# Hybrid decoder layer on one core: the second tile's x and rows loaded one per step, the attention bias begun at another point

## The chip, the cores and the metric

The kernel runs on one core of a Trainium2 chip. The metric is the device time of one execution in microseconds (us). The core has five engines that run their own instruction streams: TensorE (PE, with weight loads listed apart as PEld), VectorE (DVE), ScalarE (ACT), GpSimd (POOL) and SyncE (SP), the last of which issues most of the DMA transfers here. Lines such as L127 are lines of the kernel's file before the change.

## The reference

One decoder layer on x of 2048 positions and 1024 channels, all float32:

```
hn   = rms_norm(x, mix_pre_g)
proj = hn @ w_in                       # 1024 -> 1792: q, k, v and u
attn = sliding_window_attention(q, k, v, attn_sinks, rel_bias)   # window 128, 8 heads of 64
conv = conformer_conv(u, ...)          # GLU, causal conv of 31 taps, layer norm, swish, pointwise
h    = x + rms_norm(concat(attn, conv) @ w_out, mix_post_g)
hf   = rms_norm(h, ffn_pre_g)
out  = h + rms_norm((silu(hf @ w_gate) * (hf @ w_up)) @ w_down, ffn_post_g)
```

The bias of attention is rel_bias (32 buckets by 8 heads) picked by the distance of query and key.

## The kernel before

**Precision.** Each float32 operand of a large product is split in a high half (an ACT copy to fp32r) and a low half (a subtraction on POOL or DVE), and each product is three products on PE: high by high, high by low, low by high (`three`, `split_w`).

**Tiles and stages.** The 2048 positions are four tiles of 512. Stage A (labels A0 to A3, `stage_a`) is the first projection of a tile: 14 units of 128 output columns, each of 8 blocks of 128 channels by three products, so 24 products of 128x512. Units 0 to 7 are the GLU pairs of the four convolution groups, 8 and 9 are k and v, 10 to 13 are q. Stage C (`stage_taps`) does the 31 convolution taps on DVE; stage B is attention; stages W, F, H and G are the output projection and the FFN. X (`stage_x`) makes the attention bias once; U (`stage_fold`) folds the pointwise weights into the output weights.

**How a unit's weights come.** `kweight` loads 512 KB of w_in into a tile of tag raw (two buffers), splits it in two halves (tag w, six buffers, so three units), and in the first tile stores the low halves to a scratch tensor lo_in (two stores of 256 KB), from which the later tiles read them. In the first tile units 0 to 5 are subtracted on POOL (`TAPS0 = 6`), the rest on DVE.

**How x comes.** The first tile's transposed x (label X0) is loaded at the very start. For the second tile, step 2 of A0 calls `h1`, which is `load_x`: four DMAs of 512 KB (tag x, four buffers, L262). Step 4 calls `h0`, which is `row_norms`: four DMAs of 512 KB of the rows of x (tag p, L276), a Square with a running sum on ACT for each (L277), and `rsqrt`, three small DVE instructions and twelve small ones on POOL (L153 to L156). Step 8 (`h2`) makes the diagonal matrix of the norms, step 10 (`h3`) transposes and copies it, steps 11 and 12 (`h4`, `h5`) scale and split the eight blocks of x for stage A1 (tags mid and chl).

**What sets the order.** The code below is emitted in program order with a priority; a planner then orders each engine's stream, SP's included, by that priority and a model of when the operands are ready. An instruction may thus stand in its stream far ahead of its place in the code when its buffers are free. A manual dependency marked NoSync orders two instructions in the plan and puts no semaphore between them; `tied` puts one on the last product so far. Side stages run in lanes: after every unit the main loop yields its cost (5.2) and `pump` gives each lane credit for it, at 0.8 for lane lb, with X first and B0 to B3 behind it. A lane's stage takes its next part when its credit is above zero, and its yields are taken off the credit. X starts when its condition holds, here that the second tile's x has been begun (`"x1" in started`).

Of the kernel before, what the change touches and what calls it, by code (L numbers as in the profile page):

```python
# [17 lines left out]
AF = mybir.ActivationFunctionType  # L18
# [5 lines left out]
D = 1024  # L24
DFF = 2816
P = 128
T = 512
# [10 lines left out]
def layer_kernel(ctx, tc, x, xT, cols, rows, sinks, relb, onehot, w_in, w_pw, w_out, w_gate, w_up, w_down, out):  # L38
    nc = tc.nc
# [7 lines left out]
    lab = ["X0"]  # L47

    def nm(s):
        uid[0] += 1  # L50
        return f"{s}@{lab[0]}_{uid[0]}"
# [3 lines left out]
    def t_(tag, shape, dt=F32):  # L55
        return sb.tile(list(shape), dt, tag=tag, name=nm(tag), bufs=BUFS[tag])

    def f4(tag, shape=(P, D)):
        return t_(tag, shape)

    def f2(tag, shape=(P, T)):
        return t_(tag, shape)
# [4 lines left out]
    def sm(n, dt=F32):  # L67
        kind = "A" if lab[0][0] == "G" else lab[0][0]
        return sb.tile([P, 8], dt, tag="sm" + kind, name=nm("sm"), bufs=16)[:, 0:n]
# [9 lines left out]
    act = nc.scalar.activation  # L79
# [4 lines left out]
    def mat(*args, **kw):  # L84
        r = nc.tensor.matmul(*args, **kw)  # L85
        if made["new"]:
            made.update(rows=[], at=0, new=False)
        made["rows"].append(r.ins)
        return r
# [54 lines left out]
    def rsqrt(ssq, n, mean_over, beside_taps=True):  # L144
        v = sm(n)
        y = sm(n)
        t = sm(n)
        vts(v, ssq, 1.0 / mean_over, EPS, ALU.mult, ALU.add)
        vts(y.bitcast(I32), v.bitcast(I32), 1, None, ALU.logical_shift_right)
        vts(y.bitcast(I32), y.bitcast(I32), -1, 0x5F3759DF, ALU.mult, ALU.add)  # L150
        for _ in range(3):
            if beside_taps:
                ptt(t, y, y, ALU.mult)  # L153
                ptt(t, t, v, ALU.mult)
                nc.gpsimd.tensor_scalar(t, t, -0.5, 1.5, ALU.mult, ALU.add)
                ptt(y, t, y, ALU.mult)  # L156
            else:
                vtt(t, y, y, ALU.mult)
                stt(t, v, -0.5, t, ALU.mult, ALU.mult)
                stt(y, t, 1.5, y, ALU.add, ALU.mult)  # L160
        return y
# [20 lines left out]
    def tied(r):  # L182
        tc.add_manual_dep(
            r.ins,
            made["rows"][-1].name,
            mybir.DependencyInfo(mybir.DependencyClass.NoSync, mybir.DependencyReason.DATA),
            reason="keeps pace with the products",
        )
        return r
# [56 lines left out]
    junk = cst.tile([P, D], BF16, name="junk")  # L246
# [8 lines left out]
    started = set()  # L255
# [9 lines left out]
        return [xs]  # L265

    rn = {}

    def row_norms(ts, tag):
        lab[0] = f"A{ts[0]}"  # L270
        n = 4 * len(ts)
        ssq = sm(n)
        for i in range(n):
            xt = f4(tag)
            r0 = ts[0] * T + i * P
            nc.sync.dma_start(xt, x[r0 : r0 + P])  # L276
            act(junk, xt, AF.Square, accum_out=ssq[:, i : i + 1])  # L277
        r = rsqrt(ssq, n, D)
        for j, t in enumerate(ts):
            rn[t] = r[:, 4 * j : 4 * j + 4]  # L280
# [13 lines left out]
    def norm_x(t, xs, acc):  # L294
        lab[0] = f"A{t}"
        bank_of = mm if t else ct
        if t:
            r = acc
        else:
            o = bank_of()  # L300
            for s in range(4):
                mat(o[:, s : s + 1], acc[:, s * P : (s + 1) * P], ones, start=True, stop=True)
            r = rsqrt(o[:, 0:4], 4, D, False)
        dg = f2("gb")
        for s in range(4):
            vts(dg[:, s * P : (s + 1) * P], ident, 0.0, r[:, s : s + 1], ALU.mult, ALU.add)
        yield
        lab[0] = f"A{t}"
        o = bank_of()
        for s in range(4):  # L310
            nc.tensor.transpose(o[:, s * P : (s + 1) * P], dg[:, s * P : (s + 1) * P], ident)
        rb = f2("gb")
        act(rb, o, AF.Copy)
        yield rb
# [336 lines left out]
    def stage_fold():  # L651
        lab[0] = "U0"

        def two(src):
            raw = f4("wx", (P, 2, T))
            nc.sync.dma_start(raw, src)
            return raw

        wp = []
        for i in range(2):  # L660
            lab[0] = "U0"
            raw = two(w_pw[2 * i : 2 * i + 2].rearrange("c p t -> p c t"))
            wp += [split_w(raw[:, j], "mid", on_pool=False) for j in range(2)]
            yield 2.76
        for n in range(2):
            wo = []
            for i in range(2):
                lab[0] = "U0"
                c = 4 + 2 * i
                raw = two(w_out[c : c + 2, :, n * T : (n + 1) * T].rearrange("c p t -> p c t"))  # L670
                wo += [split_w(raw[:, j], "chl", on_pool=False) for j in range(2)]
                yield 0.1 if n else 2.76
            for m in range(4):
                lab[0] = "U0"
                o = mm()
                ms = slice(m * P, (m + 1) * P)
                three(o, [((wp[j][:, 0, ms], wp[j][:, 1, ms]), (wo[j][:, 0], wo[j][:, 1])) for j in range(4)])
                f = hl("chl" if m % 2 else "mb")
                act(f[:, 0], o, AF.Copy)
                vtt(f[:, 1], o, f[:, 0].bitcast(F32), ALU.subtract)  # L680
                nc.sync.dma_start(fold[n, m], f.bitcast(F32))
                yield 2.76
# [3 lines left out]
    def stage_x():  # L686
        lab[0] = "X0"
        rel = cst.tile([32, 8], F32, name="rel")
        nc.sync.dma_start(rel, relb)
        oh = f2("fa", (P, 2 * P))  # L690
        nc.sync.dma_start(oh[0:32], onehot)
        pb = tr()
        mat(pb[0:8, 0 : 2 * P], rel, oh[0:32], start=True, stop=True)
        bs = f2("fa", (P, 2 * P))
        nc.vector.tensor_copy(bs[0:8], pb[0:8, 0 : 2 * P])
        b_scr = dr.tile([8, 2 * P], F32, name="b_scr")
        nc.sync.dma_start(b_scr, bs[0:8])
        yield 8
        lab[0] = "X0"
        flip = f2("fa", (P, P))  # L700
        nc.gpsimd.memset(flip, 0.0)
        nc.gpsimd.affine_select(
            out=flip, in_=flip, compare_op=ALU.not_equal, fill=1.0, base=1 - P, pattern=[[1, P]], channel_multiplier=1
        )
        up = t_("mb", (P, 8, P))
        nc.sync.dma_start(up, bass.AP(tensor=b_scr.tensor, offset=b_scr.offset, ap=[[1, P], [2 * P, 8], [1, P]]))
        yield 8
        lab[0] = "X0"
        t = t_("mb", (P, 8, P))
        for n in range(2):  # L710
            o = tr()
            mat(o, flip, up[:, 4 * n : 4 * n + 4].rearrange("p h k -> p (h k)"), start=True, stop=True)
            nc.vector.tensor_copy(t[:, 4 * n : 4 * n + 4].rearrange("p h k -> p (h k)"), o)
        bias.append(t)
        yield 0.1
# [673 lines left out]
    lb = Lane(RB, 0)  # L1389
# [19 lines left out]
    def mark(gen, name):  # L1409
        for c in gen:  # L1410
            yield c
            started.add(name)

    lb.add("X", stage_x(), lambda: "x1" in started)
    lu.add("U", stage_fold(), lambda: "A2" in started)
    lw.add("W0", stage_w(0, "x", ["hl"] * 4, ["wx"] * 4, mm), lambda: "A3" in started and "C0" in ld.done and "U" in lu.done)
    TGA = [["hl"] * 8, ["mid"] * 4 + ["chl"] * 4, ["hl"] * 8, ["mid"] * 4 + ["hl"] * 4]
    xa = {}
# [8 lines left out]
    for t in range(NT):  # L1427
        hooks = {}
        if t + 1 < NT:

            def h1(t=t + 1):
                xa[t] = load_x(t)

            def h3(t=t + 1):
                xa[t][2] = next(xa[t][2])

            def h4(t=t + 1):
                hn_a[t] = split_x(t, xa[t][0], xa[t][2], range(4))

            def h5(t=t + 1):  # L1440
                hn_a[t] += split_x(t, xa[t][0], xa[t][2], range(4, KC))

            def h0(t=t + 1):
                row_norms([t] if t == 1 else [2, 3], "p" if t == 1 else "hl")

            def h2(t=t + 1):
                xa[t] += [rn[t], norm_x(t, xa[t][0], rn[t])]
                next(xa[t][2])

            if t == 0:  # L1450
                hooks = {2: h1, 4: h0, 8: h2, 10: h3, 11: h4, 12: h5}
            elif t == 1:
                hooks = {0: h1, 2: h0, 7: h2, 9: h3, 10: h4, 11: h5}
            else:
                hooks = {H1: h1, H2: h2, H3: h3, H4: h4}
        run(mark(stage_a(t, hn_a[t], (lambda: lb.until(f"B{t-1}")) if t else (lambda: None), hooks,
                         None if t else norm_x(0, x0, sum_squares(0, x0))), f"A{t}"))
        lb.add(f"B{t}", stage_b(t))
        if t == 2:
            hn_a[t + 1] += split_x(t + 1, xa[t + 1][0], xa[t + 1][2], range(4, KC))  # L1460
# [97 lines left out]
```

## Time and profile before

| | us |
|---|---|
| median of 3 runs (1934.53 to 1942.58) | 1941.39 |
| the profiled execution | 1939.15 |
| its span in the profile | 1937.4 |
| PE busy in the span | 1897.0 |
| DVE busy in the span | 1475.7 |
| ACT busy in the span | 959.2 |
| POOL busy in the span | 310.2 |

The views of the profile are read like this. In a view of stretches each row is a stretch of the span with the busy time of each engine in it (and how many instructions), then the granted clock of TensorE as a share of full speed, the busy share of the DMA engines and the GB/s that they moved. In a view by time a row is the start, the duration, the engine, the line, the operation, the tile written and the tiles read, the shapes, the count, and in brackets how long the engine sat idle before it and what it waited for. In the view of waits a row is who waited for whom, with the total, the number of times and the longest. SPq marks what SP's queue issues. Between the label A0's first products and its last stand about 90 us of the span; the first large matrix product starts at 7.08 us.

### The profile page before, as it was taken

The page shows a single profiled execution, that of the slowest core. Times are in us where ns is not written, and L with a number is a line of the kernel's source. Part 1 is how long each engine was busy: PE and PEld are TensorE (multiplying, and loading weights), DVE is VectorE, ACT ScalarE, POOL GpSimd, SP SyncE. Part 2 cuts the span into 40 slices and gives each one's busy share as a digit, 9 for nine tenths or more (in the row PEclk, how much of TensorE's full clock was granted, in tenths as well). Part 3 has the DMA queues.
Part 4 walks back from the last instruction along what each step waited for, and adds up shares of the span by engine and source line. Part 5 has one row for each costly group of instructions (what it writes and reads, how often), then busy time and mean ns, then how long its engine had stood idle before and what let it go on. Part 6 is the DMA issues. An engine that isn't in the chain of part 4 may idle for free.

```text
span 1937.4 us, 26679 instructions
## 1 busy us (share of the span) xinstructions
PE 1897.0 (98%) x8730; PEld 1532.9 (79%) x8730; DVE 1475.7 (76%) x2648; ACT 959.2 (50%) x1886; POOL 310.2 (16%) x451
## 2 busy tenths in 40 slices
PE   8999999999999999999999999999999999999997
PEld 6777777677777888787888788888788888888886
DVE  4999979995986997888669964678777766455557
ACT  5365465446748533333454555567534333345453
POOL 4010121011120011211000110002033333211003
PEclk9999999999999999999999999999999999999998
DMA  8787766657758667777577875769745443375663
GB/s 306 244 307 232 229 200 237 212 192 226 255 190 308 232 231 259 250 262 239 172 256 245 305 270 196 247 232 361 262 153 167 153 147 114 115 262 187 201 202 138
DMA packets 208556, 435.68 MB, mean 225 GB/s; under 512 B 21753, under 2 KB 39329, under 8 KB 208417
## 3 DMA queue, kind: packets, MB, share of 16 engines
q1 hardware_dynamic: 188192, 394.13, 60.8%
q0 software_dynamic: 9472, 31.46, 4.7%
q10 hardware_dynamic: 10752, 8.39, 1.3%
q8 instruction: 68, 1.11, 0.2%
q14 instruction: 72, 0.58, 0.1%
HBM read 323.26 MB, written 110.63 MB: 224 GB/s over the span
## 4 chain that ended last, share of the span: by engine, by line
PE 66%; DVE 15%; DMA 12%; issue 3%; ACT 2%; POOL 2%; SPq 0%; DVEq 0%; ACTq 0%; POOLq 0%
PE mm@F L85 30%; PE mm@G L85 17%; PE mm@A L85 8%; DVE fc@C L94 5%; PE mm@W L85 4%; PE tr@W L85 3%; PE tr@B L85 2%; DMA mids<-fa@F 2%; DMA chl@H<-hT 1%; DMA fc@G<-w_down 1%; DMA raw@A<-w_in 1%; DVE w@F L94 1%; DVE fa@F L94 1%; DVE chl@F L94 1%; DMA mixT<-yt@C 1%
## 5 line engine op out<-in xcount | busy, mean ns | idle before, releaser
L94 DVE SCALAR_TENSOR_TENSOR fc@C<-glu@C,colt,fc@C 128x512 f32<-128x512 f32 x480 | 361.2, 768 | 2.7
L85 PE MATMUL mm@F<-hl@H,w@F 128*128 128x512 f32 x1056 | 256.8, 393 | 7.2 <-ACT w@F L850 4.0
L85 PEld LDWEIGHTS mm@F<-hl@H,w@F 128*128 128x128 f32 x1056 | 198.0, 189 | 52.6 <-ACT w@F L850 5.3
L85 PE MATMUL mm@G<-hl@G,hl@G 128*128 128x512 f32 x924 | 227.5, 393 | 2.2 <-DVE hl@G L94 2.2
L850 ACT ACTIVATE w@F<-chl@F 128x512 fp32r<-128x512 f32 x220 | 135.7, 626 | 175.9 <-PE mm@F L85 144.6
L85 PE MATMUL mm@A<-hl@A,w@A 128*128 128x512 f32 x840 | 209.2, 397 | 5.1 <-ACT w@A L127 2.8
L85 PEld LDWEIGHTS mm@G<-hl@G,hl@G 128*128 128x128 f32 x924 | 171.5, 188 | 38.9 <-DVE hl@G L94 3.3
L85 PE MATMUL mm@G<-w@G,hl@G 128*128 128x512 f32 x876 | 199.4, 389 | 0.0
L85 PEld LDWEIGHTS mm@A<-hl@A,w@A 128*128 128x128 f32 x840 | 156.1, 189 | 44.7 <-issue 3.9
L85 PEld LDWEIGHTS mm@G<-w@G,hl@G 128*128 128x128 f32 x876 | 164.4, 188 | 34.1
L94 DVE TENSOR_TENSOR w@F<-chl@F,w@F 128x512 fp32r<-128x512 f32 x198 | 152.9, 777 | 46.2 <-ACT w@F L850 46.0
L85 PE MATMUL mm@F<-mid@H,w@F 128*128 128x512 f32 x528 | 132.1, 390 | 1.0 <-DVE fa@F L94 0.5
L85 PE MATMUL mm@F<-ql@H,w@F 128*128 128x512 f32 x528 | 130.0, 390 | 0.0
L85 PE MATMUL mm@F<-p@H,w@F 128*128 128x512 f32 x528 | 129.1, 389 | 0.0
L85 PE MATMUL mm@F<-x@H,w@F 128*128 128x512 f32 x528 | 125.9, 391 | 0.0
L85 PEld LDWEIGHTS mm@F<-mid@H,w@F 128*128 128x128 f32 x528 | 99.0, 188 | 22.3 <-DVE fa@F L94 1.0
L85 PEld LDWEIGHTS mm@F<-x@H,w@F 128*128 128x128 f32 x528 | 98.7, 188 | 21.3 <-issue 0.8
L85 PEld LDWEIGHTS mm@F<-p@H,w@F 128*128 128x128 f32 x528 | 99.1, 188 | 20.6
L85 PEld LDWEIGHTS mm@F<-ql@H,w@F 128*128 128x128 f32 x528 | 98.8, 188 | 20.2
L516 POOL TENSOR_SCALAR_AFFINE_SELECT p@B<-p@B 128x512 f32<-128x512 f32 x62 | 56.1, 911 | 339.6 <-ACT p@B L514 338.0
L127 ACT ACTIVATE w@A<-raw@A 128x512 fp32r<-128x512 f32 x110 | 67.4, 626 | 85.5 <-PE mm@A L85 53.2
L94 DVE TENSOR_TENSOR w@G<-raw@G,w@G 128x512 fp32r<-128x512 f32 x73 | 53.4, 731 | 71.4 <-ACT w@G L850 70.5
(320 smaller groups left out, 3253.3 us busy)
## 6 DMA issues: line engine op xcount, KB each, us to landing
mids<-fa@F SPq DMA_DIRECT2D x154, 256.0 KB, 2.9
raw@A<-w_in SPq DMA_DIRECT2D x55, 512.0 KB, 4.6
w@A<-lo_in SPq DMA_DIRECT2D x84, 256.0 KB, 3.7
fc@G<-mids SPq DMA_DIRECT2D x77, 256.0 KB, 3.3
fa@G<-mids SPq DMA_DIRECT2D x75, 256.0 KB, 4.5
w@W<-fold SPq DMA_DIRECT2D x32, 512.0 KB, 5.7
gb@F<-keeps SPq DMA_DIRECT2D x54, 256.0 KB, 3.9
chl@F<-w_gate SPq DMA_DIRECT2D x22, 512.0 KB, 5.1
```

Of the source, the lines that this page charges most:

```text
L85: r = nc.tensor.matmul(*args, **kw)
L94: r = op(*args, **kw)
L127: act(w[:, 0], raw, AF.Copy)
L516: cut = nc.gpsimd.affine_select(out=pg[:, kb].rearrange("p (i q) -> p i q", q=P), in_=pg[:, 1].rearrange("p (i q) -> p i q", q=P), compare ...
L850: act(w[:, 0], x, AF.Copy)
```

## The change

Three things are changed, all in the first tile and around it.

- A new generator `first_norms` takes the place of `load_x` and `row_norms` for the second tile. It is called at steps 1 to 8 of A0. Steps 1 to 4 issue one row load each, steps 5 to 8 one block of transposed x each, every DMA tied to the last product emitted so far. The Square of a row is emitted one step after its load. `rsqrt` is emitted at step 7 in place of step 4.
- X waits for `"g00" in started` (the first GLU group of the first tile is done) in place of `"x1" in started`.
- X yields 6 between its load of the one-hot table and its first product, where there was no pause, and 10 in place of 8 before its last part. Its yields sum to 24.1 in place of 16.1.

Buffers, tags and the arithmetic are the same, as are `h3`, `h4` and `h5`. The calls of the later tiles are the same.

```
+    def first_norms():
+        xs, rows_ = [], []
+        ssq = sm(4)
+        for i in range(4):
+            lab[0] = "A1"
+            rows_.append(f4("p"))
+            tied(nc.sync.dma_start(rows_[i], x[T + i * P : T + (i + 1) * P]))
+            if i:
+                act(junk, rows_[i - 1], AF.Square, accum_out=ssq[:, i - 1 : i])
+            yield
+        for i in range(4):
+            lab[0] = "A1"
+            xs.append(f4("x", (P, 2, T)))
+            tied(nc.sync.dma_start(xs[i], xT[2 * i : 2 * i + 2, :, T : 2 * T].rearrange("c p t -> p c t")))
+            if i == 0:
+                act(junk, rows_[3], AF.Square, accum_out=ssq[:, 3:4])
+            if i == 2:
+                rn[1] = rsqrt(ssq, 4, D)
+            if i == 3:
+                xa[1] = [xs]
+            yield
+        yield
...
         oh = f2("fa", (P, 2 * P))
         nc.sync.dma_start(oh[0:32], onehot)
+        yield 6
+        lab[0] = "X0"
         pb = tr()
...
-        yield 8
+        yield 10
         lab[0] = "X0"
         t = t_("mb", (P, 8, P))
...
-    lb.add("X", stage_x(), lambda: "x1" in started)
+    lb.add("X", stage_x(), lambda: "g00" in started)
...
             if t == 0:
-                hooks = {2: h1, 4: h0, 8: h2, 10: h3, 11: h4, 12: h5}
+                early = first_norms()
+                h = lambda: next(early)
+
+                def h2(t=t + 1):
+                    h()
+                    xa[t] += [rn[t], norm_x(t, xa[t][0], rn[t])]
+                    next(xa[t][2])
+
+                hooks = {1: h, 2: h, 3: h, 4: h, 5: h, 6: h, 7: h, 8: h2, 10: h3, 11: h4, 12: h5}
```

## The prediction

> **What bounds the kernel now.** I read the page's first lines, then equal stretches of 40 us, then PE's waits and the chain in the first tile.
>
> ```profile
> span 1937.4 us, 26679 instructions
> ...
> PE 1897.0 (98%) x8730; PEld 1532.9 (79%) x8730; DVE 1475.7 (76%) x2648; ACT 959.2 (50%) x1886; POOL 310.2 (16%) x451
> ```
>
> ```profile
> 0.00:40.00 40.00, 33.27 (x148) 26.11 (x149) 19.24 (x45) 22.61 (x35) 17.68 (x29) 0.96 0.89 315
> 40.00:80.00 40.00, 38.72 (x166) 30.50 (x165) 33.55 (x55) 11.27 (x19) 6.44 (x9) 1.00 0.78 254
> 80.00:120.00 40.00, 39.24 (x193) 31.69 (x191) 39.86 (x77) 23.41 (x43) 0.00 (x0) 1.00 0.86 314
> ...
> 360.00:400.00 40.00, 36.16 (x187) 27.37 (x186) 39.75 (x96) 12.92 (x38) 5.01 (x6) 1.00 0.65 209
> ```
>
> PE is the bound: it idles 1937.4 - 1897.0 = 40.4 us in all. The change acts in the first 120 us, where PE idles 6.73 + 1.28 + 0.76 = 8.8 us and the clock falls once (0.96 in the first row). Its direct gain is therefore small beside the span.
>
> ```profile
> PE mm@A L85 <- ACT w@A L127: 2.8, 1, 2.8
> ...
> PE tr@X L85 <- DMA mb@X<-b_scr: 1.3, 1, 1.3
> ...
> PE mm@A L85 <- POOL w@A L129: 0.2, 1, 0.2
> ```
>
> These are PE's waits up to 120 us that the change can reach: one of 2.8 us for the high half of a unit's weights, 0.2 behind it for the low half, and 1.3 in X for its transfer. The others there are for the first tile's x, which is not changed. The chain of waits names the cause of the first:
>
> ```profile
> 13.15 8.43 DMA x@A<-xT
> 21.59 10.35 DMA raw@A<-w_in
> ```
>
> The weights of unit 3 were issued at 21.59 us, the instant a block of the second tile's x landed, and took 10.35 us to come. SP's queue by time and the transfers up to 45 us show the company:
>
> ```profile
> 11.30 0.38 SPq L262 DMA_DIRECT2D x@A<-xT  x1
> ...
> 18.88 1.27 SPq L131 DMA_DIRECT2D lo_in<-w@A  x2
> 20.30 0.38 SPq L262 DMA_DIRECT2D x@A<-xT  x1
> 21.59 0.33 SPq L137 DMA_DIRECT2D raw@A<-w_in  x1
> ...
> 36.82 0.32 SPq L366 DMA_DIRECT2D glu_scr<-fa@A  x1
> ```
>
> ```profile
> raw@A<-w_in SPq DMA_DIRECT2D x7, 512.0 KB, 6.0
> ...
> x@A<-xT SPq DMA_DIRECT2D x4, 512.0 KB, 10.4
> p@A<-x SPq DMA_DIRECT2D x4, 512.0 KB, 9.5
> ```
>
> Eight loads of 512 KB that nobody needs before step 8, 4.2 MB, were issued from 11.30 to 20.30 us, far ahead of their steps 2 and 4. They held the weights' issue and shared their transfer.
>
> **The change part by part.** *The eight loads.* They move from that burst to one per unit. The products' own rows give the unit and the gap:
>
> ```profile
> 29.30 0.60 PE L311 MATMUL ct@A<-ident,gb@A 128*128 128x128 f32 x4
> 32.71 1.13 PE L85 MATMUL mm@A<-hl@A,w@A 128*128 128x512 f32 x2 [2.80 <-ACT w@A L127]
> ...
> 83.09 16.58 PE L85 MATMUL mm@A<-hl@A,w@A 128*128 128x512 f32 x72
> 99.51 3.34 PE L85 MATMUL mm@A<-mid@A,w@A 128*128 128x512 f32 x14
> ```
>
> ```profile
> 16.77 5.98 POOL L129 TENSOR_TENSOR w@A<-raw@A,w@A 128x512 fp32r<-128x512 f32 x4 [7.02 <-ACT w@A L127]
> ...
> 35.50 1.29 POOL L365 TENSOR_TENSOR fa@A<-fa@A,gb@A 128x512 f32<-128x512 f32 x1
> ```
>
> A product is 16.58 / 72 = 0.230 us and a unit of 24 is 5.53. Unit 3's raw buffer is free when POOL has half of its four subtractions behind it, about 19.8; SP is past the two lo_in stores at 18.88 + 1.27 = 20.15. So the issue goes to about 20.3, and with the median landing of 6.0, an ACT half of 0.6 and a POOL half of 1.3 the weights stand at 28.2. PE wants them at 29.9 and the low half at 30.4: 2.2 us to spare, and the gap of 2.80 + 0.22 = 3.0 goes. If the landing stays 10.35 the low half is ready at 32.5 and 2.1 of it remain; so this term lies between 0.9 and 3.0, and I take 3.0, since the transfers that made 10.35 are those that move.
>
> *The clock behind the gap.* Stretches of one microsecond:
>
> ```profile
> 32.00:33.00 1.00, 0.29 (x1) 0.30 (x2) 0.00 (x0) 0.98 (x2) 0.27 (x1) 0.92 0.71 285
> 33.00:34.00 1.00, 0.84 (x2) 0.12 (x1) 0.27 (x1) 0.69 (x2) 1.00 (x2) 0.50 0.30 119
> 34.00:35.00 1.00, 0.94 (x2) 0.83 (x3) 1.00 (x2) 0.00 (x0) 1.00 (x3) 0.50 0.18 72
> 35.00:36.00 1.00, 1.00 (x4) 0.72 (x3) 0.01 (x1) 0.74 (x2) 1.00 (x3) 0.50 0.58 225
> 36.00:37.00 1.00, 1.00 (x5) 0.83 (x4) 0.00 (x0) 1.00 (x2) 0.95 (x2) 0.88 0.88 291
> ```
>
> Lost speed is 0.08 + 3 x 0.50 + 0.12 = 1.7 us, of which about 0.1 fell on idle time: 1.6 us, gone with the gap (0 if a gap of that length remains). [...]
>
> *Squares, rsqrt, the diagonal.* Their number is unchanged.
>
> ```profile
> 26.84 1.06 ACT L277 ACTIVATE junk<-p@A 128x1024 bf16<-128x1024 f32 x1 [1.47 <-DMA p@A<-x]
> ...
> 32.02 1.15 ACT L127 ACTIVATE w@A<-raw@A 128x512 fp32r<-128x512 f32 x2 [1.49 <-DMA raw@A<-w_in]
> 33.08 0.61 ACT L357 ACTIVATE fa@A<-fa@A 128x512 f32<-128x512 f32 x1
> ```
>
> A Square stands in ACT's stream and waits there for its row; queued behind it are the splits of weights and the GLU's tanh. Later in A0 the weights are two units ahead, so I cost those waits at nothing; without that cover each costs its wait (1.47 in the row). The twelve POOL instructions of rsqrt leave the stretch in which POOL splits units 3 to 5. They now run when DVE has taken over the subtractions; the diagonal behind them is DVE's and is not wanted before step 10.
>
> *Crowding later.* The loads now fall in stretches that were less full.
>
> ```profile
> 24.00:32.00 8.00, 5.90 (x32) 4.78 (x31) 3.95 (x20) 2.99 (x6) 0.79 (x4) 1.00 1.04 402
> ...
> 40.00:50.00 10.00, 10.00 (x45) 7.67 (x43) 5.01 (x11) 2.37 (x5) 4.78 (x8) 1.00 0.81 255
> 50.00:60.00 10.00, 10.00 (x46) 8.28 (x45) 9.48 (x14) 2.70 (x5) 1.66 (x1) 1.00 0.96 293
> ```
>
> One load per unit is 524 KB / 5.53 us = 95 GB/s more: 350 and 388 GB/s, under the 402 that the full stretch carried. I take nothing for it; the cover is the two units of weights ahead, and the bound is a second gap like the first, 4.6 us. [...]
>
> *SP.* Eight issues of 0.38 us each are moved behind weight loads, lo_in stores and GLU transfers; SP's stream has the room. The x blocks of step 8 are wanted at step 11, 3 x 5.53 us later, above the 10.4 that one took in the burst.
>
> *X.* The table's load stands a step ahead of the product that reads it, so that product and the b_scr store come earlier or stay, while the last part is a step later. That gives the bias's transfer more time before the two products: the 1.3 us wait goes. Bounds: 0, and a gain of 1.3. Nothing waits for the bias before stage B0, after A0's last unit.
>
> *Hand-over to the second tile.* With PE 3.0 + 1.6 + 1.3 = 5.9 us earlier, the blocks of A1 are wanted earlier.
>
> ```profile
> 97.39 1.90 DVE L94 TENSOR_TENSOR mid@A<-x@A,mid@A 128x512 fp32r<-128x512 f32 x3
> ```
>
> The first of these three ends at about 98.0 and is read by the fourth product of A1, at 99.51 + 3 x 0.23 = 100.2: 2.2 us to spare. DVE is full from there back to 61 us (39.86 of 40 in the third stretch), so it must start earlier itself. Its taps wait for the first GLU block, stored at 36.82 after POOL's 35.50. There tanh stood behind the late split (32.02), and POOL behind unit 3's subtractions; with those done, the store comes some 3.4 us sooner (tanh, two elementwise steps and POOL's 1.29 from 30.5). So 5.9 - 2.2 - 3.4 = 0.3, say 0.4 us, is waited for; bounds 0 and 3.7 (no shift of DVE).
>
> **Sum:** 3.0 + 1.6 + 1.3 - 0.4 = 5.5 us less. The profiled span goes from 1937.4 to about 1931.9; its execution took 1939.15, 2.2 below the median, so the median goes from 1941.39 to **1935.9**.
>
> **The rivals.** *A, the gap stays.* The first row's Square could stand ahead of unit 3's split in ACT's stream. Its load is issued after unit 1's products, about 23, and with the 9.5 us of p@A lands at 32.5, as late as the weights today. For it: ACT took Squares before that split in the trace. Against it: without the burst a load has 6.0, and the plan may put the split first. Then only X's 1.3 is left: 1940.1.
>
> *B, slower: the weights run late from unit 4 on.* The place is the two raw buffers. A buffer's round is landing, 0.6 on ACT, 2.6 on POOL or DVE and 0.4 on SP; two buffers feed PE if it is below 2 x 5.53 = 11.06, so this decides from a landing of 7.5 us. With the 10.35 of the burst the round is 13.95, or 7.0 per unit: 1.45 late in each of units 4 to 11, 11.6 us, and a clock drop of 1.6 at every second one, 6.4. Less the 5.5: 12.5 slower, 1953.9. For it: a DMA share of 0.96 already at 293 GB/s. Against it: the median of 6.0 was taken with the burst in it.
>
> *C, the gain carries further.* DVE sets two waits later on:
>
> ```profile
> PE tr@B L85 <- DVE sm@A L94: 1.2, 1, 1.2
> ...
> PE mm@W L85 <- DVE x@W L94: 2.5, 1, 2.5
> ```
>
> The first is at 120 us, the second is most of the 3.84 us idle between 360 and 400. Taps begun earlier, and another order of the planner behind them, could take both: 5.5 + 1.2 + 3.8 = 10.5, or 1930.9. Against it: the order of the later stages need not move, and could also lose such a gap.
>
> **How the numbers follow.** Forecast 0.50, A 0.14, B 0.12, C 0.24. About 0.5%, or 9.7 us, is what a measurement of this kernel can tell from no change (the three runs lie 8 apart). Faster needs less than 1931.7: most of C, 0.19, and 0.04 from the forecast's lower end, 0.23. Slower needs over 1951.1: B, 0.10, and 0.02 from a bad order later. The same holds 0.65. The range 1927 to 1946 takes in the forecast, A and C with a few microseconds of the runs' spread and leaves B out.
>
> **What would show it.** The x and row loads spread over steps 1 to 8; unit 3's weights landing before 29 us; no PE wait near 30 and a clock of 1.00 from 30 to 40; no wait of tr@X; PE's first product of A1 near 94 us. Wrong would be a PE wait of 2 us at unit 3 behind a Square (A), landings of raw above 7.5 us with repeated waits (B), or a change in the stages behind 400 us larger than that before 120 us.

## The result and the profile after

The changed kernel took a median of 1948.47 us (7 runs, 1947.38 to 1954.48) beside 1936.23 us for the kernel before in the same series (7 runs, 1931.67 to 1942.58). The ratio over the rounds is 1.0056 with a 95% interval of 1.0038 to 1.0073: slower by about 11 us, where 5.5 us less were forecast. The profiled execution took 1948.31 us. First the head of its page:

```profile
span 1946.6 us, 26680 instructions
...
PE 1901.1 (98%) x8730; PEld 1537.1 (79%) x8730; DVE 1473.0 (76%) x2648; ACT 958.2 (49%) x1886; POOL 311.4 (16%) x451
```

The span grew by 9.2 us. PE idles 1946.6 - 1901.1 = 45.5 us, 5.1 more than before, and is busy 4.1 longer with the same 8730 instructions: some of them ran at a lower clock. In stretches of 20 us up to 800 us the granted clock is below 1.00 once before (0.91 from 20 to 40 us) and five times after (0.91, 0.98 and 0.94 in the first 60 us, 0.91 from 120 to 140 and from 380 to 400 us). Stretches of 40 us, as shown of before:

```profile
0.00:40.00 40.00, 33.86 (x154) 27.59 (x155) 19.97 (x42) 21.13 (x32) 17.63 (x21) 0.95 0.78 259
40.00:80.00 40.00, 40.00 (x167) 31.69 (x166) 32.73 (x56) 13.16 (x23) 6.89 (x17) 0.97 0.93 320
80.00:120.00 40.00, 37.52 (x184) 30.34 (x183) 37.01 (x70) 23.33 (x43) 0.00 (x0) 1.00 0.88 316
```

The transfers moved as meant: the first row's 315 GB/s fell to 259, the second's 254 rose to 320. PE's waits up to 120 us:

```profile
PE mm@A L85 <- ACT w@A L127: 2.5, 1, 2.5
PE mm@A L85 <- DVE fa@A L94: 2.3, 1, 2.3
```

The wait of tr@X is gone. The 2.5 us for w@A are not the old wait of unit 3 but a new one at 117 us, in A1. The 2.3 us for DVE's fa@A are new as well. The same stretch on ACT, PE and DVE, by time:

```profile
25.76 1.15 ACT L127 ACTIVATE w@A<-raw@A 128x512 fp32r<-128x512 f32 x2 [5.28 <-DMA lo_in<-w@A]
...
32.01 1.06 ACT L277 ACTIVATE junk<-p@A 128x1024 bf16<-128x1024 f32 x1
...
37.01 0.58 ACT L336 ACTIVATE gb@A<-ct@A 128x512 f32<-128x512 f32 x1
```

```profile
26.70 7.79 PE L85 MATMUL mm@A<-hl@A,w@A 128*128 128x512 f32 x33
34.33 0.60 PE L334 MATMUL ct@A<-ident,gb@A 128*128 128x128 f32 x4
34.68 1.41 PE L85 MATMUL mm@A<-hl@A,w@A 128*128 128x512 f32 x5
38.37 8.01 PE L85 MATMUL mm@A<-hl@A,w@A 128*128 128x512 f32 x27 [2.28 <-DVE fa@A L94]
...
97.92 3.56 PE L85 MATMUL mm@A<-mid@A,w@A 128*128 128x512 f32 x15
```

```profile
30.91 0.88 DVE L94 TENSOR_SCALAR gb@A<-ident,sm@A 128x128 f32<-128x128 f32 x4
37.62 0.69 DVE L94 TENSOR_TENSOR fa@A<-mm@A,gb@A 128x512 f32<-128x512 f32 x1 [5.83 <-ACT gb@A L336]
...
56.36 0.54 DVE L94 TENSOR_SCALAR fc@C<-glu@C,colt 128x512 f32<-128x512 f32 x1
```

The weights of unit 3 are split at 25.76 in place of 32.02, ahead of the first Square (32.01), and 33 products run without a gap. But the four transposes of the first tile's norms (L334) now stand behind 19 products of unit 3. Before, they stood between units 2 and 3, at 29.30. Their diagonal was ready at 30.91 + 0.88 = 31.8, so from then on they waited for nothing but their place in PE's stream. Behind them comes the whole chain of the first tile: ACT's copy of the norms to gb (37.01, before at 29.94), DVE's multiplication by it (37.62), which also frees PE's banks, and the GLU. DVE idled 5.83 us for it, and PE stood 2.28 us for a bank.

The place in PE's stream is not the whole delay, though. The copy comes 7.1 us later than before, in three parts. The diagonal itself is 2.3 us late (31.8, before at 29.5): two small DVE instructions ahead of it took 1.96 us in place of 0.38, at the time at which POOL now subtracts unit 3's weights. First the row of before, then two of the changed kernel:

```profile
26.35 0.38 DVE L94 TENSOR_SCALAR sm@A<-sm@A 128x4 int32<-128x4 int32 x2
```

```profile
27.07 1.96 DVE L94 TENSOR_SCALAR sm@A<-sm@A 128x4 int32<-128x4 int32 x2
```

```profile
26.47 2.54 POOL L129 TENSOR_TENSOR w@A<-raw@A,w@A 128x512 fp32r<-128x512 f32 x2 [3.04 <-ACT w@A L127]
```

The transposes add 2.7 us (they end at 34.93, before at 29.90), and ACT's copy another 2.0, since it stands behind the split of unit 5's weights (35.95 to 37.10). SP's queue by time shows the end of the chain:

```profile
25.46 0.45 SPq L275 DMA_DIRECT2D p@A<-x  x1
...
41.09 0.34 SPq L389 DMA_DIRECT2D glu_scr<-fa@A  x1
...
61.56 1.06 SPq L282 DMA_DIRECT2D x@A<-xT  x2
```

The first GLU store stands at 41.09, 4.3 us later than the 36.82 of before, and the first tap on DVE at 56.36 in place of 45.64. Only 4.3 of these 10.7 us are the store's. The block is loaded back at 49.26, 8.2 us behind its store (3.7 before), and the tap stands in DVE's stream behind the second tile's `rsqrt` and diagonal, for which DVE waited 2.84 and 0.49 us on POOL.

For the whole span a view of growing stretches is read by its counts: the number in brackets behind PE's busy time says how many products (transposes among them) PE had begun by then. Before, then after:

```profile
0.00:80.00 80.00, 71.99 (x312) 56.61 (x313) 52.79 (x100) 33.88 (x53) 24.12 (x37) 0.98 0.83 284
...
0.00:400.00 400.00, 386.63 (x1910) 300.47 (x1911) 351.40 (x767) 199.63 (x464) 65.00 (x97) 1.00 0.73 244
0.00:680.00 680.00, 664.64 (x3263) 519.07 (x3264) 579.92 (x1218) 376.60 (x838) 104.27 (x189) 1.00 0.72 240
```

```profile
0.00:80.00 80.00, 73.86 (x319) 59.28 (x320) 52.71 (x97) 34.29 (x54) 24.52 (x37) 0.96 0.86 290
...
0.00:400.00 400.00, 386.90 (x1896) 302.06 (x1897) 349.36 (x766) 199.61 (x463) 62.69 (x97) 0.98 0.73 241
0.00:680.00 680.00, 657.96 (x3212) 513.28 (x3213) 568.67 (x1201) 370.09 (x827) 103.20 (x187) 0.99 0.72 237
```

At 80 us the changed kernel is 319 - 312 = 7 products ahead, 7 x 0.23 = 1.6 us. At 400 us it is 14 behind (3.2 us), at 680 us 51 behind (11.7 us). So the loss arises between 80 and 680 us, in stages that the change doesn't touch. The lead at 80 us is no gain: two more kernels with the start of before, before_rate and before_pause below, stand 1.6 and 1.3 us ahead of this trace of before there too. PE's waits from 120 to 700 us name the places:

```profile
PE mm@F L85 <- ACT mm@F L993: 3.9, 3, 1.5
PE tr@B L85 <- DVE sm@B L497: 3.1, 1, 3.1
...
PE tr@B L85 <- POOL p@B L539: 2.2, 1, 2.2
PE ct@H L870 <- ACT gb@H L871: 1.6, 1, 1.6
```

None of these four stands in the trace of before at that size: there the long waits of that stretch are 2.5 us of mm@W for DVE's x@W, 1.7 in all of mm@F for ACT and 1.2 of tr@B. What the planner does behind the first tile has changed; from 780 us of before on (791 in the changed kernel) PE's stream is the same again, operation for operation. One such wait doesn't mark a slow kernel: x_alone below, which lost nothing, has 3.6 us for sm@B.

### The profile page after: what moved, and what is told of

Its sections match the earlier page's. It is cut to its first block, busy times and chain, and to the rows that moved or that the text cites. A ratio compares the mean times of both kernels' runs of the same rounds, so it can differ in the third digit from the quotient of the medians.

```text
span 1946.6 us, 26680 instructions
## 1 busy us (share of the span) xinstructions
PE 1901.1 (98%) x8730; PEld 1537.1 (79%) x8730; DVE 1473.0 (76%) x2648; ACT 958.2 (49%) x1886; POOL 311.4 (16%) x451
## 4 chain that ended last, share of the span: by engine, by line
PE 67%; DVE 12%; DMA 11%; issue 4%; ACT 3%; POOL 2%; SPq 0%; DVEq 0%; POOLq 0%; ACTq 0%
PE mm@F L85 32%; PE mm@G L85 18%; PE mm@A L85 7%; PE tr@W L85 4%; DVE fc@C L94 4%; PE mm@W L85 2%; PE tr@B L85 1%; DMA chl@H<-hT 1%; DMA raw@A<-w_in 1%; DMA mixT<-yt@C 1%; DMA w@A<-lo_in 1%; DMA mids<-fa@F 1%; DVE x@W L94 1%; DMA yt@W<-mixT 1%; DMA fc@G<-w_down 1%
## 5 line engine op out<-in xcount | busy, mean ns | idle before, releaser
L94 DVE SCALAR_TENSOR_TENSOR fc@C<-glu@C,colt,fc@C 128x512 f32<-128x512 f32 x480 | 354.0, 757 | 2.2
L85 PE MATMUL mm@F<-hl@H,w@F 128*128 128x512 f32 x1056 | 257.1, 393 | 9.0 <-ACT w@F L875 4.0
L85 PEld LDWEIGHTS mm@F<-hl@H,w@F 128*128 128x128 f32 x1056 | 198.1, 189 | 54.5 <-ACT mm@F L993 6.4
L85 PE MATMUL mm@G<-hl@G,hl@G 128*128 128x512 f32 x924 | 227.5, 393 | 3.0 <-DVE hl@G L94 3.0
L85 PE MATMUL mm@A<-hl@A,w@A 128*128 128x512 f32 x840 | 208.5, 398 | 4.5 <-DVE fa@A L94 2.3
L85 PEld LDWEIGHTS mm@G<-hl@G,hl@G 128*128 128x128 f32 x924 | 171.5, 188 | 39.7 <-DVE hl@G L94 4.0
L85 PE MATMUL mm@G<-w@G,hl@G 128*128 128x512 f32 x876 | 199.4, 389 | 0.0
L85 PEld LDWEIGHTS mm@A<-hl@A,w@A 128*128 128x128 f32 x840 | 158.2, 191 | 42.6 <-issue 3.1
L85 PEld LDWEIGHTS mm@G<-w@G,hl@G 128*128 128x128 f32 x876 | 164.5, 188 | 34.1
L85 PE MATMUL mm@F<-mid@H,w@F 128*128 128x512 f32 x528 | 131.9, 389 | 0.4 <-DVE w@F L94 0.4
L85 PE MATMUL mm@F<-ql@H,w@F 128*128 128x512 f32 x528 | 129.2, 390 | 0.7 <-ACT w@F L875 0.7
L85 PE MATMUL mm@F<-p@H,w@F 128*128 128x512 f32 x528 | 129.1, 389 | 0.0
L85 PE MATMUL mm@F<-x@H,w@F 128*128 128x512 f32 x528 | 125.8, 390 | 0.0
L85 PEld LDWEIGHTS mm@F<-mid@H,w@F 128*128 128x128 f32 x528 | 99.0, 188 | 21.4 <-DVE w@F L94 0.9
L85 PEld LDWEIGHTS mm@F<-ql@H,w@F 128*128 128x128 f32 x528 | 98.7, 188 | 21.2 <-ACT w@F L875 1.1
L85 PEld LDWEIGHTS mm@F<-p@H,w@F 128*128 128x128 f32 x528 | 99.1, 188 | 20.6
L85 PEld LDWEIGHTS mm@F<-x@H,w@F 128*128 128x128 f32 x528 | 98.7, 188 | 21.1 <-issue 0.8
```

The source lines that it names most:

```text
L94: r = op(*args, **kw)
```

## The experiments

Two theories stood against each other. **Late start:** the transposes behind 19 products delay the GLU and the taps, and this delay is carried to the end. **Order:** the edit leads the planner to another order of everything behind it, and that order is what costs, however the start went. A third question is which of the two edits, loads or X, does it.

For each run I also took from its trace the time at which PE had done a given share of its product columns, less the time at which the kernel before had done it. This finer form of the counts above is called the lag. The second column says behind how many products of unit 3 the four transposes stand.

```
run                      transposes  ratio   95% interval     lag at 80   400    680   end
after                    19          1.0056  1.0038-1.0073    -1.6    3.1   11.5    9.3
x_alone                   0          0.9991  0.9982-1.0001    -1.6    1.8    1.0   -3.0
loads_alone              19          1.0065  1.0050-1.0079    -1.7   12.2   11.9   12.4
transposes_early          6          0.9986  0.9975-0.9996    -1.6   -2.5   -3.4   -5.4
transposes_late          14          1.0053  1.0035-1.0071     3.2   13.6   15.2   12.4
change_then_old_order    19          1.0028  1.0014-1.0042    -2.7    4.6    4.3    5.5
before_then_new_order     0          1.0056  1.0044-1.0068    -1.4    2.6   10.8   11.8
early_then_old_order      6          1.0029  1.0018-1.0040    -4.3    3.3    3.1   -0.3
transposes_at_15         15          1.0018  1.0007-1.0028    -5.8    5.0    7.0    1.7
before_rate               0          0.9996  0.9986-1.0006    -1.6   -0.4    0.9   -3.8
before_pause              0          1.0000  0.9990-1.0010    -1.3   -0.9   -0.6   -2.0
after_rate               19          1.0022  1.0012-1.0033    -1.2   -4.5    6.5    2.9
after_pause              19          1.0017  1.0007-1.0026    -2.0    0.1    6.1    4.8
```

A lag comes from one profiled execution and scatters: no engine's stream differs between after and after_pause before 520 us, yet the lags differ by 3.0 us at 400. Its zero scatters too. before_rate and before_pause have the streams of before up to some 155 and 520 us, and are 1.6 and 1.3 us ahead of its trace at 80; so a lag of about -1.5 at 80 us is the level of the old start, and not a lead. The ratios come from repeated runs.

### The two edits apart

The edit of x_alone, on the kernel before (loads as before):

```diff
+        yield 6
+        lab[0] = "X0"
...
-        yield 8
+        yield 10
...
-    lb.add("X", stage_x(), lambda: "x1" in started)
+    lb.add("X", stage_x(), lambda: "g00" in started)
```

> The kernel before with the change's X alone (its condition and its pauses). Theory: the 9 us come from the order of the first tile's norm transposes on PE, which the loads bring about, not X. So X alone takes away at most its own wait of 1.3 us: 1935 to 1938 where the kernel before has 1936, and the transposes stay ahead of unit 3. Rival, X: its parts now stand elsewhere in the streams and cost the time: 1945 or more.

It took 0.9991 of before, with 1.0 inside the interval. The wait of tr@X is gone from its list of PE's waits, and no loss comes of X. What X gains isn't shown: the lag at 80 us is -1.6, but before_rate has -1.6 with the old X.

The edit of loads_alone, on the changed kernel (X as before, with its condition met at step 2, as before):

```diff
+            if i == 1:
+                started.add("x1")
...
-        yield 6
-        lab[0] = "X0"
...
-        yield 10
+        yield 8
...
-    lb.add("X", stage_x(), lambda: "g00" in started)
+    lb.add("X", stage_x(), lambda: "x1" in started)
```

> The changed kernel with X's old pauses, X begun at step 2 as before: the loads alone. Theory: nearly the whole loss is here, 1944 to 1950, with the transposes of the first norm behind 19 products of unit 3 and the first tap after 54 us. Rival, X: 1932 to 1937.

It took 1.0065: the loads carry the whole loss. The start is that of the changed kernel (transposes at 34.16 behind 19 products, a PE wait of 2.37 for DVE's fa@A), but the way there is another one: it lost 7 us between 120 and 200 us, with a wait of 5.46 us of mm@A for DVE's ql@A, 7 more between 300 and 400, and stayed level from 400 us on. Its first tap began at 50.78, not after 54 us as I had expected. Already this speaks for a later order that is different each time.

### The transposes moved

The edit of transposes_early, on the changed kernel: the seventh product of unit 3 is ordered behind the last transpose.

```diff
+        if ahead["on"]:
+            after_first(ahead["tr"], r)
+            ahead["on"] = False
...
-            nc.tensor.transpose(o[:, s * P : (s + 1) * P], dg[:, s * P : (s + 1) * P], ident)
+            ahead["tr"] = nc.tensor.transpose(o[:, s * P : (s + 1) * P], dg[:, s * P : (s + 1) * P], ident)
...
+                ahead["on"] = t == 0 and u == 3 and k == 2
```

> The changed kernel with the four transposes of the first norm ordered ahead of the third block of unit 3 (behind 6 of its products in place of 19). Theory: PE no longer runs out of banks near 36 us, the first tap comes before 50 us in place of 56, and the lag that grows from 40 to 680 us goes: 1930 to 1936. Rival, crowded transfers: weights land late whatever the order of PE, 1945 to 1950. Rival, the planner's order of later stages: it need not heal, 1940 to 1950 although the taps start early.

It took 0.9986, interval 0.9975 to 0.9996: 0.7% under the changed kernel and slightly under the kernel before. PE by time:

```profile
26.78 4.84 PE L87 MATMUL mm@A<-hl@A,w@A 128*128 128x512 f32 x20
32.65 0.30 PE L339 MATMUL ct@A<-ident,gb@A 128*128 128x128 f32 x1 [1.03 <-DVE gb@A L99]
33.78 0.72 PE L339 MATMUL ct@A<-ident,gb@A 128*128 128x128 f32 x3 [0.83 <-DVE gb@A L99]
```

PE now waits 1.9 us for the diagonal, and the wait for a bank is gone. The first tap still began at 55.91, not before 50 as I had expected. So late taps alone do not make the kernel slow: with the taps as late as in the changed kernel, this one is 2.4 us behind at 200 us, but 2.5 ahead at 400 and 3.4 at 680. Nor do earlier taps make it fast: loads_alone has them at 50.78. The theory of the late start lost its carrier here.

The edit of transposes_late, on the kernel before: the loads stay, the transposes go behind 14 products of unit 3.

```diff
-            nc.tensor.transpose(o[:, s * P : (s + 1) * P], dg[:, s * P : (s + 1) * P], ident)
+            r = nc.tensor.transpose(o[:, s * P : (s + 1) * P], dg[:, s * P : (s + 1) * P], ident)
+            if t == 0:
+                tc.add_manual_dep(
+                    r.ins,
+                    made["rows"][-11].name,
...
+                oa = proj(3)
...
-            half.send(proj(2 * c + 1))
+            half.send(oa if oa is not None else proj(2 * c + 1))
```

> The kernel before, loads in their burst, with the transposes forced behind 14 products of unit 3. Theory: PE keeps its first gap, GLU and taps start as late as in the changed kernel, so it loses as much or more: 1943 to 1955. Rivals (X, crowded transfers): neither is in this kernel, so 1936 to 1939.

It took 1.0053, as slow as the change, with the loads of before: unit 3 is emitted ahead of the transposes, these stand at 34.96, and PE waits 4.17 us for DVE's fa@A. Its lag is 3.2 us at 80 us and 13.6 at 400. This start suffices, then, with the loads of before; but most of the loss again comes behind 80 us. It isn't one of late transposes alone. ACT's copy of the norms was done at 36.85, and the multiplication began only at 41.31, since the second tile's diagonal now stands ahead of it on DVE: four instructions that took 0.87 us in before took 4.96 here (36.43 to 41.39). PE's wait of 4.17 us is theirs. That late transposes by themselves suffice is therefore not shown. That the delay itself is carried, or that it leads to another order, these four runs can't tell apart.

### The order pinned

In the next three kernels the start is left as it is in one kernel, and everything emitted from the second tile's norm diagonal on (step 8 of A0; 14044 of 14529 instructions) is held, engine by engine, in the planned order of the other. The edges are NoSync, so they order the plan and put no semaphore. The table of orders stands at the file's head, which shifts the line numbers (L106 is L85 of the kernels before and after).

```diff
+    for e, blob in PLAN.items():
...
+        for a, b in zip(order[:-1], order[1:]):
+            tc.add_manual_dep(
+                ins[b],
+                ins[a].name,
+                mybir.DependencyInfo(mybir.DependencyClass.NoSync, mybir.DependencyReason.DATA),
```

The kernel before's start with the changed kernel's later order:

> The reverse: the kernel before up to step 8 of A0, with its burst of loads and its early transposes, and the changed kernel's order behind it. Late start: 1935 to 1939. Later order: 1944 to 1950.

It took 1.0056, interval 1.0044 to 1.0068: the whole loss, though loads, X and transposes (29.66) stand as before and the first tap begins at 45.25. Its growing stretches, and its PE waits from 120 to 700 us:

```profile
0.00:80.00 80.00, 73.05 (x319) 57.89 (x320) 54.15 (x102) 34.53 (x54) 24.67 (x37) 1.00 0.82 284
...
0.00:400.00 400.00, 385.17 (x1899) 300.12 (x1900) 348.16 (x768) 200.33 (x465) 64.06 (x97) 1.00 0.72 241
0.00:680.00 680.00, 657.84 (x3216) 512.46 (x3217) 566.95 (x1201) 371.10 (x828) 104.66 (x187) 0.99 0.71 237
```

```profile
PE tr@B L106 <- DVE sm@B L495: 3.7, 1, 3.7
PE mm@F L106 <- ACT mm@F L989: 2.9, 3, 1.2
PE tr@B L106 <- POOL p@B L537: 2.4, 1, 2.4
```

The counts are those of the changed kernel within 4 products, and the three waits are its waits (3.1, 3.9 and 2.2 there). The order alone puts them there. From 131 us on PE's stream is that of the changed kernel, operation for operation, and every engine has as many instructions as in the two kernels. No run pinned a kernel to its own order, so what pinning itself might cost was not measured; the trace gives no sign of it.

The changed kernel's start with the later order of the kernel before:

> The changed kernel whose planned order of everything emitted from step 8 of A0 on (14044 of 14529 instructions, on all five engines) is tied by NoSync edges to that of the kernel before; its own start stays, with the transposes behind 19 products of unit 3. Theory, late start: the late transposes make GLU and taps late, and lateness alone costs the later stalls: 1944 or more. Rival, the planner's later order: the traces of both kernels stand 1.6 us apart in the change's favour at 80 us, so with the old order behind it the kernel takes 1932 to 1938.

It took 1.0028, between the two theories. PE's waits from 120 to 700 us:

```profile
PE tr@B L106 <- DVE sm@A L115: 2.7, 1, 2.7
PE mm@W L106 <- DVE x@W L115: 2.1, 1, 2.1
PE mm@F L106 <- ACT mm@F L1014: 1.2, 1, 1.2
```

Here are the waits of the kernel before (x@W 2.5, one of mm@F 1.2 in its trace), and those of the changed kernel are gone. Its lag went from -2.7 at 80 us to 3.1 at 120 us, where PE stood 3.27 us for DVE's taps (ct@C) and then 2.72 us for sm@A; from there on it stayed between 3 and 5.5. From 117 us on PE's stream is that of the kernel before. Is that loss of 6 us the late start, or an old order that doesn't fit a new start? The start of transposes_early, which took 0.9986 with its own order, followed by the order of before:

> The changed kernel with the transposes behind 6 products of unit 3, and the order of the kernel before from step 8 on. Both theories: at or below the kernel before; if starts and orders add up, 1932 to 1936.

It took 1.0029, not the 1932 to 1936 us I had expected, with the same two waits in the same places (2.83 us of ct@C, 1.15 of tr@B). A start that is good for 0.9986 with its own order is worth 1.0029 with a borrowed one. So the 0.28% of change_then_old_order is at least in part a misfit of start and order. The trace names it: the first taps began at 56.58 and 53.38 us, against 45.64 in before, so DVE wasn't through when PE came to the products of the taps (ct@C) at their old place. As measures of the start alone these two runs fail. What stands is that the long loss from 120 to 680 us isn't in them.

### Is it late transposes or luck of the order

The edit of transposes_at_15 is that of transposes_early with `k == 5` in place of `k == 2`: the transposes behind 15 products.

> The changed kernel with the transposes behind 15 products of unit 3 (6 gave 1935, 19 give 1948), order behind them left to the planner. Late start: the loss grows with the place, so 1941 to 1946. Later order: whatever order the planner comes to, anything from 1932 to 1950, without regard to the place.

It took 1.0018, with no PE wait for a bank and a lead of 5.8 us at 80 us, the largest of all. It went at once into waits for the second tile's weights (w@A from lo_in, 1.41 us at 111 and 2.38 at 117), and by 400 us it is 5.0 behind. The best start of all ends behind the kernel before: the lead at 80 us decides nothing.

Then edits that should do nothing, on each kernel: a lane's rate of credit, which in the traces first moves a stream at about 155 us (before) and 161 us (after), and a pause, which first moves one at about 520 us in both, and PE's at 571 and 577. The expectations put these places too early (130 and 390 us).

```diff
-    RC0, RC1, RC2, RC3, RW0, RW, RB, LC = 0.7, 1.1, 0.4, 0.9, 1.7, 1.25, 0.8, 100
+    RC0, RC1, RC2, RC3, RW0, RW, RB, LC = 0.7, 1.1, 0.4, 0.9, 1.7, 1.25, 0.84, 100
```

```diff
-    YC = 3
+    YC = 3.2
```

> The kernel before with lane lb's rate at 0.84 in place of 0.80: nothing of the change, and the plan first differs behind the 727th product, near 130 us. It asks how far planned orders scatter by themselves. If the later order is the cause and its quality is chance, this may land anywhere from 1930 to 1950; if only the change makes bad orders, 1934 to 1940.

> The kernel before with attention's pause YC at 3.2 in place of 3: the plan is the same for 2700 products, to about 390 us, and differs up to the 6315th, about 1370 us. Chance: its lag against the kernel before is zero up to 390 us and then moves by several us either way.

> The changed kernel with the same rate, its first 809 products planned as in the change. Chance: anything from 1932 to 1950. The change itself, through its start, always leads to a bad order: 1945 to 1950.

> The changed kernel with the same pause, the plan the same up to 2692 products. The lag of the change grows from 3 us at 400 to 11 at 640. Chance: that growth is another one here, so 1938 to 1948. The change's own start makes it: 8 us again between 400 and 640, 1946 to 1950.

On the kernel before they took 0.9996 and 1.0000, on the changed kernel 1.0022 and 1.0017. So about 0.2% stays with the change under both nudged orders, and some 0.35% of the 0.56 is the particular order that it happened to get: nudging a rate by 5% takes it away. The growth of the lag between 400 and 680 us stayed in both, with 11.0 and 6.0 us. At 500 us, before the pause moves a stream, after_pause was 7.0 us behind and the change 7.5; behind it they part, to 4.8 and 9.3 at the end.

The nudges on the kernel before also show what the forecast was sized on. before_rate has its old start:

```profile
31.40 0.73 PE L85 MATMUL mm@A<-hl@A,w@A 128*128 128x512 f32 x2 [1.22 <-ACT w@A L127]
...
60.30 1.95 PE L85 MATMUL tr@X<-mb@X,fa@X 128*128 128x512 f32 x4 [0.41 <-DMA mb@X<-b_scr]
...
97.92 3.33 PE L85 MATMUL mm@A<-mid@A,w@A 128*128 128x512 f32 x14
```

Unit 3's gap is 1.22 us for the high half and 0.63 for the low one, X's wait is 0.41, and A1 begins at 97.92, as in the changed kernel.

## Why the prediction was wrong, point by point

**The burst and the first gap: right.** The row loads and blocks of x spread from 25.46 to 61.56 us; unit 3's weights are no longer late; PE was 4.3 us ahead at 40 us, where 3.0 + 1.6 = 4.6 were forecast. The 3.0 was one execution's: in before_rate and before_pause the gap is 1.9 and 2.1 us, with a granted clock of 0.98 over the first 80 us, as in before. x_alone, which leaves the burst, keeps the gap (2.25 us for w@A and 0.62 for its low half), so the gap does come from the burst. Rival A isn't seen: the first Square stands behind unit 3's split.

**X: right in the mechanism, its size not shown.** The wait is gone and no loss comes of it. But the 1.3 us was one execution's: with the old X the wait is 0.4 us in before_rate and 0.3 in before_pause, so with the gap the three terms come to about 4 us there, and not 5.9.

**Crowding: right to take nothing.** No wait for w@A repeats from unit 4 on, so rival B's mechanism didn't occur. The outcome is on rival B's side by another way.

**The hand-over: wrong, and the first failed step.** "So the store comes some 3.4 us sooner": it came 4.3 us later. That sentence moved tanh and POOL's steps forward with the weights and left the norm transposes where they were. But they share PE's stream with unit 3, whose products became plannable earlier and were put ahead of them. The sum of 3.4 us started at 30.5, where ACT's copy of the norms ended before; that copy now began at 37.01, by the transposes' place, by the diagonal's 2.3 us and by ACT's own order. Of the 5.9 us ahead by the forecast's terms 1.6 were left at 80 us, and none against before_rate: the bank wait of 2.28 us, and 0.41 + 2 x 0.50 + 0.30 = 1.7 us lost to the clock behind it, took back what the gap had given. In stretches of one microsecond of the changed kernel:

```profile
38.00:39.00 1.00, 0.63 (x3) 0.55 (x4) 0.31 (x1) 0.63 (x1) 1.00 (x1) 1.00 0.67 268
39.00:40.00 1.00, 1.00 (x5) 0.77 (x4) 0.99 (x2) 0.49 (x1) 0.39 (x2) 0.59 0.67 226
40.00:41.00 1.00, 1.00 (x4) 0.81 (x3) 1.00 (x2) 1.00 (x3) 1.00 (x1) 0.50 1.06 308
41.00:42.00 1.00, 1.00 (x4) 0.81 (x3) 1.00 (x2) 0.18 (x1) 0.07 (x1) 0.50 0.75 258
42.00:43.00 1.00, 1.00 (x4) 0.76 (x4) 0.81 (x2) 0.00 (x0) 0.11 (x1) 0.70 0.97 287
```

The forecast removed one gap with its clock drop and didn't see that the same stretch would make another. PE's first product of A1 stands at 97.92 accordingly, 1.6 us before the 99.51 of before, and not near 94. transposes_at_15, which has neither the bank wait nor that fall of the clock (1.00 granted over its first 80 us, against 0.96 in the changed kernel), begins A1 at 93.74: there the first 80 us went as forecast, and the time still wasn't gained.

**`rsqrt`: costed at nothing, and not free in place.** The forecast let its POOL instructions run later because the diagonal isn't wanted before step 10. In DVE's stream they stand ahead of the first tap, which came 10.7 us late. That this costs time at the end isn't shown: transposes_early has the tap as late and is not slow.

**The order behind the change: wrong, and the larger part.** "The order of the later stages need not move, and could also lose such a gap" stood beside rival C as an argument against a gain. It moved, and it lost: from 1.6 us ahead at 80 us to 11.5 behind at 680. The prediction's own sign of being wrong, a change behind 400 us larger than that before 120, came true: 8.4 us from 400 to 680, against 0.2 behind at 120. That this order makes the loss is shown by before_then_new_order: the old start with the new order costs 1.0056, with the same waits in the same places. The forecast gave such a loss a few hundredths; no rival had it as its mechanism.

**Late transposes and the order.** Of the kernels that follow the planner throughout, the six with the transposes behind 14 products or more took 1.0017 to 1.0065, the four with them behind 6 or none 0.9986 to 1.0000. The theory of a late start in its simple form, a delay that is carried on, falls: at 80 us all kernels but transposes_late are level with the old start or ahead of it, transposes_early has its taps as late as the change, and transposes_at_15 has the best start and still loses. Why the planner finds poorer orders behind late transposes wasn't settled: six kernels against four are a pattern, not a mechanism (three of the six share one start, and transposes_late delays more than its transposes), and none of the runs looked into the planner's choices between 120 and 400 us one by one.

## What to carry to other kernels

Where a planner orders the streams, an edit that brings one load forward reorders what shares the stream: look at which small instructions at the head of a chain (here four transposes of 0.15 us) get pushed behind products that have become ready sooner, and tie them to their place. Compare the planned order of everything behind an edit before a gain at its place is believed, and pin it to find out whether place or order made the time. Size a wait by more than one execution: the two waits that the forecast removed were 4.3 us in the trace that it read, and 2.3 and 2.4 in two others of the same start. A single result of such a kernel carries the luck of its later order (here some 0.3%), so try a few neutral nudges of each version before one is kept.

## What the runs showed of the hardware that was not expected

In these traces the clock's fall did not follow the length of PE's gap where gaps were near 2 us. The changed kernel's gap of 2.28 us (36.09 to 38.37) was followed by a granted clock of 0.59, 0.50, 0.50 and 0.70 from 39 to 43 us, shown above. The same products with much the same gap, 2.45 us (36.36 to 38.81) in change_then_old_order, went on at 1.00:

```profile
36.00:37.00 1.00, 0.36 (x2) 0.00 (x0) 0.00 (x0) 0.60 (x2) 0.00 (x0) 1.00 1.03 315
...
38.00:39.00 1.00, 0.18 (x1) 0.19 (x2) 0.69 (x1) 0.24 (x2) 1.00 (x2) 1.00 0.65 266
39.00:40.00 1.00, 1.00 (x5) 0.82 (x5) 0.54 (x1) 0.71 (x2) 0.62 (x1) 1.00 0.76 274
40.00:41.00 1.00, 1.00 (x6) 0.79 (x5) 1.00 (x3) 1.00 (x3) 0.77 (x1) 1.00 0.65 227
```

Two shorter gaps in a row, 1.03 and 0.83 us in transposes_early, were followed by the fall (0.91, three times 0.50 and 0.88 from 34 to 39 us, 1.7 us lost), and 0.80 and 0.89 us in early_then_old_order were not (1.00 in each microsecond from 30 to 48 us). So gaps of this size cost their own length alone or about 1.7 us more, and which of the two their length doesn't tell. What decides it was not shown: no run here shifted a gap in time and left the rest alone.

In the rows read here small DVE instructions took three to six times as long where POOL subtracted blocks of 128x512 beside them. The two 128x4 instructions shown above took 0.38 us in before and 0.37 in transposes_late (29.98), and 1.96 in the changed kernel, where POOL's two subtractions for unit 3 ran from 26.47 to 29.01; the two DVE instructions ended at 29.03. The four instructions of the first diagonal took 0.88 us in before and in the changed kernel, and 2.97 in loads_alone (31.08) and 2.79 in transposes_early (31.33), where POOL was busy for 2.6 and 2.5 us from 31 to 34 us. In transposes_late the second diagonal's four ran from 36.43 to 41.39, 4.96 us beside 0.87 in before, and four subtractions on POOL from 36.35 to 41.31. That POOL holds DVE up is read from times that coincide; no run moved POOL's work alone.
